# A hybrid attention and mLSTM block: GpSimd's weight work in pieces of 256 columns, fixed orders before the first feed-forward product and at the embedding gate, and a padding of 56 floats

## The chip, the cores and the metric

The kernel runs on one core of one Trainium2 chip. The metric is the device time of one execution in microseconds (us), the median of several runs. A core has five engines that are programmed apart and wait for each other by semaphores: TensorE (PE, with its weight loads shown as PEld), VectorE (DVE), ScalarE (ACT), GpSimd (POOL) and SyncE (SP), which issues transfers.

## The reference

One transformer block over 512 tokens of 1024 features, in float32. What matters here is its second half:

```python
merged = sigmoid(gate_a) * (y_a @ w_up_a) + sigmoid(gate_b) * (y_b @ w_up_b)
h = layer_norm(ALPHA * h + merged @ w_out, ln1_g, ln1_b)
ff = square(relu(h @ w_ff1)) @ w_ff2            # 1024 -> 4096 -> 1024
r = ALPHA * h + ff
r = r + sigmoid(r @ w_ple_gate) * (p @ w_ple_proj)   # the embedding gate
h = layer_norm(r, ln2_g, ln2_b)
```

Before it stand the input projection, a sparse attention with rotary embeddings, and an mLSTM, which give `y_a` and `y_b`.

## The kernel before

Every float32 product is made of three products of rounded halves. A weight or an activation `w` is cast to a high part (`wh`, on ScalarE), the low part is the difference `w - wh` (on VectorE or GpSimd: `split`, L110 to L112, and the last lines of `load_w`, L134), and `mm3` (L140 to L143) adds high x high (L141), high x low (L142) and low x high (L143) in one PSUM bank. So each tile of weights brings a transfer into a raw tile (`raw_tile`, three buffers), a cast on ScalarE, a subtraction on VectorE or GpSimd, and only then can L142 or L143 run on it.

The program has stages, one after the other on TensorE: input projection, attention and gates (to about 220 us), mLSTM (307), up projections with `merged`, here `m` (353), the output projection (`po`, weights `wo`, eight tiles in two halves `hh`) with the first layer norm and with transposes of the normed rows (`h_factors`, PSUM tiles `hps`) (405), the projection of `p` (`ple_projection`, PSUM tiles `ppw`, eight of 128x512, copied to `pws`) (418), the first feed-forward product (`ff1`, PSUM tiles `pf`, to 583), the second one (`ff2`, L1074, to 737), the embedding gate (`gate_product`, PSUM tiles `pg`, weights `wpg`, eight tiles) and the second layer norm.

Both feed-forward products use a fast scheme of seven products for eight blocks. `ff1` needs sums of blocks of the weights (`sums`, made by four GpSimd operations for each raw tile, L805 to L808 in `left_factors`), which are split into `w1h` and `w1l` like the weights, and sums of blocks of the normed rows, split into `hcH` and `hcL` by `put` in `h_factors`, L757 to L771. Its matmuls have the 128x128 blocks of `w1h` and `w1l` as stationary operands and 256 columns of `hcH` and `hcL` as moving ones. At the end of `ff2`, six GpSimd additions bring `e16` into `r` (L1110).

In the embedding gate `gate_inputs(i)` transposes the rows of block `i` (PSUM tiles `rps`) and splits them into `rH` and `rL`, and `gate_product(i, hh)` multiplies them by half `hh` of the weights; `gated` (L1201 to L1203) then applies the tanh (`th`) on ScalarE and two operations on VectorE.

What sets the order on each engine: the code is written for a framework that schedules the instructions by a simulated time, so the order on an engine is not that of the code. `tc.issue_after(...)` holds instructions behind a named one; `queued` (its operations have line L996) holds elementwise work of `ff2` and the gate in a list of its own, given out in order between the matmuls. An engine runs its list strictly in order.

```python
    def split(src, hi, lo, lo_eng=None):
        se.copy(hi, src)
        (lo_eng or ve).tensor_sub(lo, src, f(hi))
...
    gate_product(0, 0)
    for k in range(4):
        load_gate(1, k)
    gate_inputs(2)
    gate_product(1, 0)
    gate_inputs(3)
    gate_product(2, 0)
```

## Time and profile before

| | |
|---|---|
| median of 3 runs | 798.66 us (798.2 to 801.0) |
| the profiled execution's own time | 799.72 us |
| its span, first to last instruction | 798.0 us |
| TensorE busy | 776.5 us, 97% |
| VectorE, ScalarE, GpSimd busy | 614.1, 421.9, 361.4 us |
| mean granted TensorE clock | 0.989 of full speed |

Busy time is the union of an engine's instructions; matmuls are pipelined, so a matmul's own duration is longer than the distance between two starts. A wait is the idle time of an engine before an instruction, with the instruction that ended it. The granted clock is what the chip's throttle gave TensorE, 1.00 for 2.4 GHz and 0.50 for 1.2 GHz; a value between them is a mean over a stretch.

### The profile page before, as it was taken

What the parts mean: (1) busy time and instruction counts of PE and PEld (TensorE: products, weight loads), DVE (VectorE), ACT (ScalarE), POOL (GpSimd) and SP (SyncE); (2) the same over time, 40 slices, a digit from 0 to 9 for tenths busy, and PEclk for the clock granted to TensorE, in tenths of its full rate; (3) what the DMA queues carried; (4) which work ended last, traced back from release to release, by engine and by line L of the source; (5) the groups of instructions that cost most, each with busy time, mean ns of one, the idle gap of its engine ahead of it and who ended that gap; (6) DMA issues with size and microseconds to landing.
All of it is one profiled execution on the core that took longest, in us unless ns stands there. A gap on an engine that the chain in (4) does not pass through costs nothing.

```text
span 798.0 us, 11974 instructions
## 1 busy us (share of the span) xinstructions
PE 776.5 (97%) x4374; PEld 672.6 (84%) x4374; DVE 614.1 (77%) x1069; ACT 421.9 (53%) x687; POOL 361.4 (45%) x419
## 2 busy tenths in 40 slices
PE   8999999999999999999998999999999999999895
PEld 7888888779978888877888999999988888888685
DVE  4558999964548986384887889879878988989556
ACT  4445566687656543342255666566655456455300
POOL 5645563433245536475256877767410101118200
PEclk9999999999999999999999999999999999999898
DMA  7433133222222102546043366733169799893402
GB/s 223 139 80 105 54 80 91 64 71 68 66 80 80 39 28 67 180 143 231 1 172 106 120 240 180 246 117 97 49 152 213 146 403 294 143 203 111 129 27 79
DMA packets 84980, 102.06 MB, mean 128 GB/s; under 512 B 6197, under 2 KB 58933, under 8 KB 83642
## 3 DMA queue, kind: packets, MB, share of 16 engines
q1 hardware_dynamic: 74826, 80.33, 31.5%
q0 software_dynamic: 7392, 14.68, 10.6%
q10 hardware_dynamic: 2704, 6.29, 2.4%
q8 instruction: 34, 0.56, 0.3%
q14 instruction: 24, 0.20, 0.1%
HBM read 92.90 MB, written 8.39 MB: 127 GB/s over the span
## 4 chain that ended last, share of the span: by engine, by line
PE 72%; DVE 15%; POOL 5%; ACT 3%; DMA 3%; issue 2%; SPq 0%; DVEq 0%; POOLq 0%; ACTq 0%
PE pf L1074 16%; PE pf L141 6%; PE pf L143 6%; PE pf L142 6%; DVE sc L347 3%; DVE m L346 3%; PE pg L143 2%; PE pg L142 2%; PE pg L141 2%; PE po L142 2%; PE po L143 2%; PE po L141 2%; POOL r L1110 2%; PE pu L141 1%; PE pu L143 1%
## 5 line engine op out<-in xcount | busy, mean ns | idle before, releaser
L141 PE MATMUL pf<-hcH,w1h 128*128 128x256 f32 x448 | 123.0, 284 | 2.8 <-DVE hcL L112 2.5
L142 PE MATMUL pf<-hcL,w1h 128*128 128x256 f32 x448 | 123.9, 283 | 0.0
L143 PE MATMUL pf<-hcH,w1l 128*128 128x256 f32 x448 | 117.8, 283 | 0.6 <-DVE w1l L112 0.6
L141 PEld LDWEIGHTS pf<-hcH,w1h 128*128 128x128 f32 x448 | 84.7, 191 | 3.4 <-DVE hcL L112 2.7
L142 PEld LDWEIGHTS pf<-hcL,w1h 128*128 128x128 f32 x448 | 85.3, 190 | 0.0
L143 PEld LDWEIGHTS pf<-hcH,w1l 128*128 128x128 f32 x448 | 81.6, 190 | 0.8 <-DVE w1l L112 0.8
L938 POOL DMA_DIRECT2D b<-in_w_ff x14 | 18.1, 1289 | 122.3 <-DVE wl L996 111.4
L134 POOL TENSOR_TENSOR wgl<-wgr,wgh 128x256 fp32r<-128x256 f32 x64 | 50.9, 826 | 49.3 <-ACT wgh L130 49.3
L996 DVE TENSOR_TENSOR wl<-b,wh 128x2048 fp32r<-128x2048 f32 x27 | 64.0, 2370 | 8.7 <-ACT wh L996 8.7
L1074 PE MATMUL pf<-wh,ah 128*128 128x512 f32 x224 | 60.2, 391 | 0.2 <-ACT wh L996 0.2
L1074 PE MATMUL pf<-wh,al 128*128 128x512 f32 x224 | 59.9, 390 | 0.0
L112 DVE TENSOR_TENSOR w1l<-w1r,w1h 128x256 fp32r<-128x256 f32 (+1 forms) x62 | 48.4, 805 | 12.9 <-ACT w1h L111 12.9
L1074 PE MATMUL pf<-wl,ah 128*128 128x512 f32 x224 | 55.4, 390 | 0.0
L996 ACT CAST wh<-b 128x2048 fp32r<-128x2048 f32 x27 | 51.4, 1904 | 1.7 <-DMA b<-in_w_ff 1.7
L141 PE MATMUL pg<-xH,wgh 128*128 128x512 f32 x128 | 51.0, 399 | 0.0
L143 PE MATMUL pg<-xH,wgl 128*128 128x512 f32 x128 | 51.0, 398 | 0.0
L142 PE MATMUL pg<-xL,wgh 128*128 128x512 f32 x128 | 50.9, 398 | 0.0
L1074 PEld LDWEIGHTS pf<-wh,al 128*128 128x128 f32 x224 | 42.1, 188 | 8.7
L1074 PEld LDWEIGHTS pf<-wh,ah 128*128 128x128 f32 x224 | 41.8, 188 | 9.0 <-ACT wh L996 0.6
L1074 PEld LDWEIGHTS pf<-wl,ah 128*128 128x128 f32 x224 | 42.0, 188 | 8.7
L112 DVE TENSOR_TENSOR w1l<-sums,w1h 128x1024 fp32r<-128x1024 f32 x32 | 47.2, 1479 | 1.7 <-ACT w1h L111 1.7
L111 ACT CAST w1h<-w1r 128x512 fp32r<-128x512 f32 x64 | 29.7, 510 | 32.7 <-PE pf L142 32.4
(363 smaller groups left out, 2245.7 us busy)
## 6 DMA issues: line engine op xcount, KB each, us to landing
w1r<-in_w_ff SPq DMA_DIRECT2D x64, 256.0 KB, 3.1
b<-in_w_ff POOLq DMA_DIRECT2D x14, 1024.0 KB, 9.2
wgr<-in_w_in SPq DMA_DIRECT2D x16, 512.0 KB, 3.8
b<-in_w_ff SPq DMA_DIRECT2D x8, 1024.0 KB, 7.8
wor<-in_w_out SPq DMA_DIRECT2D x8, 512.0 KB, 4.4
b<-in_w_ff ACTq DMA_DIRECT2D x4, 1024.0 KB, 11.8
wpgr<-in_w_ple_gate SPq DMA_DIRECT2D x8, 512.0 KB, 7.4
xrs<-in_x SPq DMA_DIRECT2D x4, 512.0 KB, 5.1
```

What stands on the lines that cost most here:

```text
L111: se.copy(hi, src)
L112: (lo_eng or ve).tensor_sub(lo, src, f(hi))
L134: (lo_eng or ge).tensor_sub(lo[:, k:k + n], raw[:, k:k + n], f(hi[:, k:k + n]))
L141: te.matmul(ps, sh, mh, start=first, stop=False, **kw)
L142: te.matmul(ps, sh, ml, start=False, stop=False, **kw)
L143: return te.matmul(ps, sl, mh, start=False, stop=last, **kw)
L346: ve.max(m8, sc)
L347: ve.match_replace(out=sc, in_to_replace=m8, in_values=sc, imm_value=NEG_TAKEN)
L938: return ge.dma_start(out=tl, in_=rows_of(g, w), accum_op=OP.add)
L996: order_of[engine] = getattr(engine, op)(*args, **kw)
L1074: mm = te.matmul(banks[n, s], (al if kind == 1 else ah)[:, q, tok], (wl if kind == 2 else wh)[:, q], start=fresh and kind == 0 and q == 0, ...
L1110: (ge.tensor_sub if c else ge.tensor_add)(rs, rs, e16[:, s])
```

## The change

Five things change.

1. GpSimd's subtractions and additions on weights are cut into pieces of at most 256 columns: `low` in `split` (`wo`, `wp` and the first `w1l`), the `wpg` subtractions in `load_gate` (VectorE's there into two of 512), the rotary addition, and the additions of `e16` to `r`.
2. `left_factors` is divided into `left_sums` (transfer and GpSimd's sums) and `left_factors` (casts and subtractions). The first pair of sums is requested before the last rows' output projection and lies in the pool `ln`; so does the raw tile `prw`, which leaves a raw buffer free.
3. In front of `ff1` the order is fixed: four ple projections, the splits of the sums, two ple projections, the last rows' transposes, two ple projections.
4. The embedding gate's weights for the second half are requested after `gate_inputs(3)`, and `gate_inputs` casts through `queued`.
5. A tile of 56 floats (224 bytes) per partition is placed in the pool of the factors. `w1h` and `w1l` begin at 224 modulo 256 bytes before and at 0 after; `hcH` and `hcL` stay at 192.

The diff, cut to these places:

```diff
         se.copy(hi, src)
-        (lo_eng or ve).tensor_sub(lo, src, f(hi))
+        low(lo_eng or ve, lo, src, hi)
+
+    def low(eng, lo, src, hi):
+
+        if eng is not ge:
+            return eng.tensor_sub(lo, src, f(hi))
+        w = src.shape[-1]
+        for j in range(src.shape[1]):
+            for c in range(0, w, 256):
+                o = slice(c, min(c + 256, w))
+                eng.tensor_sub(lo[:, j][..., o], src[:, j][..., o], f(hi[:, j][..., o]))
...
@@ -702,7 +715,7 @@
 
     g1, be1 = row("ln1_g", ln), row("ln1_b", ln)
 
-    norm = []
+    norm, normed = [], []
...
-    loads, sums_done = [], []
-
-    def left_factors(q, half, later=None):
+    loads = []
+
+    def left_sums(q, half, pl=None):
 
         raw = raw_tile([P, 2, 2, 256], "w1r")
         for j in range(2):
             loads.append(sy.dma_start(raw[:, j], ff1_rows[:, j, half, :, q * 256:(q + 1) * 256]))
         a11, a21, a12, a22 = (raw[:, j, :, i * P:(i + 1) * P] for j in range(2) for i in range(2))
-        sums = W1S.tile([P, 4, 2, P], F32, tag="sums", bufs=2, name="sums")
+        sums = (pl or W1S).tile([P, 4, 2, P], F32, tag="sums", bufs=2, name="sums")
         ge.tensor_add(sums[:, 0], a21, a22)
         ge.tensor_sub(sums[:, 2], a11, a21)
         ge.tensor_sub(sums[:, 1], sums[:, 0], a11)
-        sums_done.append(ge.tensor_sub(sums[:, 3], a12, sums[:, 1]))
+        ge.tensor_sub(sums[:, 3], a12, sums[:, 1])
+        return raw, a22, sums
+
+    def left_factors(raw, a22, sums, lo_eng=None, later=None):
+
         hi = W1S.tile([P, 7, 2, P], F32R, tag="w1h", bufs=2, name="w1h")
         lo = W1S.tile([P, 7, 2, P], F32R, tag="w1l", bufs=2, name="w1l")
         for o, src in ((slice(0, 2), raw[:, :, :, 0:P]), (2, a22)):
-            split(src, hi[:, o], lo[:, o], ge if q == order[0] and o != 2 else ve)
+            split(src, hi[:, o], lo[:, o], lo_eng if o != 2 else ve)
         if later is None:
             split(sums, hi[:, 3:7], lo[:, 3:7])
         else:
@@ -838,6 +856,7 @@
         first_norm(i)
         if i:
             h_factors({2: 0, 1: 2}[i])
+    sums = [left_sums(order[0], half, ln) for half in range(2)]
     out_projection(NT - 1, 0)
     pTH, pTL, wp = ple_inputs()
     out_projection(NT - 1, 1)
@@ -846,30 +865,36 @@
     first_norm(NT - 1)
     later = []
     with tc.issue_after(norm[0].ins), tc.issue_after(norm[1].ins):
-        factors = [left_factors(order[0], half, later) for half in range(2)]
+        factors = [left_factors(*a, ge, later) for a in sums]
+
+    ge.memset(W1S.tile([P, 56], F32, name="off"), 0.0)
     h_factors(1)
 
-    pwss = []
+    pwss, projected, stored = [], [], []
 
     def ple_projection(i, hh):
         ps = acc("ppw")
         tok = slice(i * P, (i + 1) * P)
-        half_product(ps, lambda k: pTH[:, k, tok], lambda k: pTL[:, k, tok], blocks(wp[hh:hh + 1]))
+        projected[:] = [half_product(ps, lambda k: pTH[:, k, tok], lambda k: pTL[:, k, tok], blocks(wp[hh:hh + 1]))]
         if i == 0:
             pwss.append(gtile("pws", F32))
         pws = pwss[hh][:, i]
-        se.copy(pws, ps)
+        stored[:] = [se.copy(pws, ps)]
         sy.dma_start(pwd[:, i, hh * 512:(hh + 1) * 512], pws)
 
     todo = [(i, hh) for hh in range(2) for i in range(NT)]
     for _ in range(4):
         ple_projection(*todo.pop(0))
-    h_factors(NT - 1)
-    with tc.issue_after(last_block[0].ins):
+    with tc.issue_after(normed[0].ins), tc.issue_after(stored[0].ins):
         for a in later:
             split(*a)
-    for _ in range(4):
+    for _ in range(2):
         ple_projection(*todo.pop(0))
+    with tc.issue_after(projected[0].ins):
+        h_factors(NT - 1)
+    with tc.issue_after(turned[0].ins):
+        for _ in range(2):
+            ple_projection(*todo.pop(0))
...
                 queued(ve, "tensor_add", e16[:, s], e16[:, s], ps)
                 for i, c in ((s, 1), (2 + s, 0), (2 + s, 1)):
-                    rs = r[:, i, c * 512:(c + 1) * 512]
-                    (ge.tensor_sub if c else ge.tensor_add)(rs, rs, e16[:, s])
+                    for o in (0, 256):
+                        rs = r[:, i, c * 512 + o:c * 512 + o + 256]
+                        (ge.tensor_sub if c else ge.tensor_add)(rs, rs, e16[:, s, o:o + 256])
...
         queued(se, "copy", w[:, 0], raw)
         eng = ge if n in (2, 3, 5, 7) else ve
-        queued(eng, "tensor_sub", w[:, 1], raw, f(w[:, 0]))
-
+        for j in range(2):
+            for o in (slice(0, 256), slice(256, 512)) if eng is ge else (slice(0, 512),):
+                queued(eng, "tensor_sub", w[:, 1, j, o], raw[:, j, o], f(w[:, 0, j, o]))
...
             transpose4(ps, r[:, i, :], kk * 4)
             v = ps.rearrange("p (k q) -> p k q", k=4)
-            split(v, rH[:, kk * 4:kk * 4 + 4, tok], rL[:, kk * 4:kk * 4 + 4, tok])
+            hi = rH[:, kk * 4:kk * 4 + 4, tok]
+            queued(se, "copy", hi, v)
+            ve.tensor_sub(rL[:, kk * 4:kk * 4 + 4, tok], v, f(hi))
 
     EARLY = P5, P3
     RAW_STEPS = (0, P3, 1), (0, P6, 1), (1, P2, 0), (1, P2, 1)
@@ -1215,11 +1244,11 @@
         layer_norm(end, r[:, i, :], pw[i], g2, be2, lambda c: sy.dma_start(out_d[tok, c], pw[i][:, c]), **kw)
 
     gate_product(0, 0)
-    for k in range(4):
-        load_gate(1, k)
     gate_inputs(2)
     gate_product(1, 0)
     gate_inputs(3)
+    for k in range(4):
+        load_gate(1, k)
     gate_product(2, 0)
     for i in range(3):
```

On ScalarE before the first feed-forward product, of the kernel before (`hps` and `b12` belong to the last rows' transposes, `sums` to the first weight's factors; the last row is the last cast for it):

```order
L861 COPY pws_4494<-ppw_4506 128x512
L761 COPY b12_4465<-hps0_4455 128x512
L111 CAST hcH_3983<-hps1_4456 128x4x128
L111 CAST w1h_4382<-sums_4377 128x1024
L111 CAST hcH_3983<-hps0_4455 128x4x128
L111 CAST w1h_4396<-sums_4391 128x1024
L861 COPY pws_4494<-ppw_4515 128x512
L111 CAST hcH_3983<-hps1_4456 128x4x128
L111 CAST hcH_3983<-hps2_4471 128x4x128
L111 CAST hcH_3983<-hps3_4472 128x4x128
```

and of the changed kernel:

```order
L111 CAST w1h_4414<-sums_4304 128x1024
L111 CAST w1h_4421<-sums_4312 128x1024
L882 COPY pws_4494<-ppw_4487 128x512
L882 COPY pws_4494<-ppw_4497 128x512
L775 COPY b12_4516<-hps0_4506 128x512
L111 CAST hcH_3986<-hps1_4507 128x4x128
L882 COPY pws_4494<-ppw_4534 128x512
L111 CAST hcH_3986<-hps0_4506 128x4x128
L882 COPY pws_4494<-ppw_4543 128x512
L111 CAST hcH_3986<-hps1_4507 128x4x128
L111 CAST hcH_3986<-hps2_4522 128x4x128
```

Both casts of `w1h` from `sums` stood between the casts of `hcH`; now they stand ahead of everything on the last rows, and two copies of projections stand between the `hcH` casts.

On ScalarE at the embedding gate, of the kernel before (`rH` from `rps` is the cast of transposed rows, two for each block of rows; `wpg` from `wpgr` that of gate weights):

```order
L111 CAST rH<-rps 128x4x128
L996 CAST wpg<-wpgr 128x1024
L111 CAST rH<-rps 128x4x128 x2
L996 CAST wpg<-wpgr 128x1024 x2
L700 DMA ln_grow<-in_ln_g 128x1024
L111 CAST rH<-rps 128x4x128
L700 DMA ln_brow<-in_ln_b 128x1024
L996 CAST wpg<-wpgr 128x1024
L1201 ACTIVATE th_7828<-pg_7803 128x512
L111 CAST rH<-rps 128x4x128 x2
L1201 ACTIVATE th_7891<-pg_7866 128x512
L111 CAST rH<-rps 128x4x128 x2
```

and of the changed kernel:

```order
L1021 CAST rH<-rps 128x4x128 x3
L713 DMA ln_grow<-in_ln_g 128x1024
L1021 CAST rH<-rps 128x4x128
L713 DMA ln_brow<-in_ln_b 128x1024
L1230 ACTIVATE th_7870<-pg_7845 128x512
L1021 CAST rH<-rps 128x4x128 x2
L1230 ACTIVATE th_7913<-pg_7888 128x512
L1021 CAST rH<-rps 128x4x128 x2
L1021 CAST wpg<-wpgr 128x1024 x3
L1230 ACTIVATE th_7984<-pg_7959 128x512
L1021 CAST wpg<-wpgr 128x1024
L1230 ACTIVATE th_8013<-pg_7988 128x512
```

The casts of `wpg` for the second half stood between those of `rH` and the tanh; now they follow the last of `rH`.

On TensorE at the start of the output projection, of the kernel before (`wo_4005` and `wo_4010` are the first two weight tiles, `po_4047` and `po_4073` the first two blocks of rows):

```order
L143 MATMUL po_4047<-wo_4005,mHL_3802 128x512
L141 MATMUL po_4047<-wo_4010,mHL_3857 128x512
L141 MATMUL po_4073<-wo_4005,mHL_3802 128x512
L142 MATMUL po_4073<-wo_4005,mHL_3802 128x512
L143 MATMUL po_4073<-wo_4005,mHL_3802 128x512
L141 MATMUL po_4073<-wo_4005,mHL_3802 128x512
L142 MATMUL po_4073<-wo_4005,mHL_3802 128x512
L143 MATMUL po_4073<-wo_4005,mHL_3802 128x512
L141 MATMUL po_4073<-wo_4010,mHL_3857 128x512
L142 MATMUL po_4047<-wo_4010,mHL_3857 128x512
L143 MATMUL po_4047<-wo_4010,mHL_3857 128x512
L141 MATMUL po_4047<-wo_4010,mHL_3857 128x512
```

and of the changed kernel (`wo_4008` and `wo_4013`, `po_4068` and `po_4094`):

```order
L152 MATMUL po_4068<-wo_4008,mHL_3805 128x512
L150 MATMUL po_4068<-wo_4013,mHL_3860 128x512
L151 MATMUL po_4068<-wo_4013,mHL_3860 128x512
L152 MATMUL po_4068<-wo_4013,mHL_3860 128x512
L150 MATMUL po_4068<-wo_4013,mHL_3860 128x512
L150 MATMUL po_4094<-wo_4008,mHL_3805 128x512
L151 MATMUL po_4094<-wo_4008,mHL_3805 128x512
L152 MATMUL po_4094<-wo_4008,mHL_3805 128x512
L150 MATMUL po_4094<-wo_4008,mHL_3805 128x512
L151 MATMUL po_4094<-wo_4008,mHL_3805 128x512
L152 MATMUL po_4094<-wo_4008,mHL_3805 128x512
```

The first product with the low part of the second weight tile (L142 before, L151 after, on `wo_4010` and `wo_4013`) stood behind seven products of the second block of rows; now it stands before them.

## Rows read from the trace of the kernel before

**Rows 1.** Page, part 1: busy time, share of the span and instructions of each engine:

```profile
PE 776.5 (97%) x4374; PEld 672.6 (84%) x4374; DVE 614.1 (77%) x1069; ACT 421.9 (53%) x687; POOL 361.4 (45%) x419
```

**Rows 2.** TensorE's waits over the whole span: waiting line, what it waited for, us in total, times, longest:

```profile
PE pf L141 <- DVE hcL L112: 2.5, 1, 2.5
...
PE pg L143 <- DVE rL L112: 1.9, 1, 1.9
...
PE po L142 <- DVE wo L112: 1.8, 1, 1.8
...
PE pg L141 <- ACT rH L111: 1.1, 1, 1.1
```

**Rows 3.** Windows, TensorE: from:to, length, busy us (instructions), granted clock, DMA share, GB/s:

```profile
363.80:367.20 3.40, 3.40 (x10) 0.50 0.79 296
369.00:384.00 15.00, 15.00 (x65) 1.00 0.43 139
421.80:426.00 4.20, 4.16 (x22) 0.59 0.72 233
430.00:480.00 50.00, 50.00 (x425) 1.00 0.51 167
600.00:700.00 100.00, 100.00 (x443) 1.00 0.93 240
754.10:760.00 5.90, 5.90 (x14) 0.52 0.00 0
789.30:798.00 8.70, 0.39 (x4) 0.76 0.16 60
```

**Rows 4.** Groups of GpSimd's instructions by form: busy us, mean ns, idle before:

```profile
L134 POOL TENSOR_TENSOR mvwl<-mvwr,mvwh 128x256 fp32r<-128x256 f32 x16 | 11.3, 735 | 18.5 <-ACT mvwh L130 14.7 <-PE ptp L440 3.8
...
L134 POOL TENSOR_TENSOR aqwl<-aqwr,aqwh 128x512 fp32r<-128x512 f32 x8 | 10.6, 1345 | 12.7 <-ACT aqwh L130 12.7
...
L112 POOL TENSOR_TENSOR wo<-wor,wo 128x1024 fp32r<-128x1024 f32 x6 | 14.3, 2398 | 9.5 <-ACT wo L111 9.5
```

**Rows 5.** Timeline, output projection: start us, duration us, engine, line, operation:

```profile
351.68 1.23 DVE L112 TENSOR_TENSOR wo<-wor,wo 128x1024 fp32r<-128x1024 f32 x1 [2.48 <-ACT wo L111]
...
353.65 0.47 PE L141 MATMUL po<-wo,mHL 128*128 128x512 f32 x1
...
354.71 2.40 POOL L112 TENSOR_TENSOR wo<-wor,wo 128x1024 fp32r<-128x1024 f32 x1 [3.10 <-ACT wo L111]
...
359.39 3.31 DVE L112 TENSOR_TENSOR wo<-wor,wo 128x1024 fp32r<-128x1024 f32 x1
```

**Rows 6.** Timeline, start of the first feed-forward product:

```profile
419.53 1.04 ACT L111 CAST w1h<-sums 128x1024 fp32r<-128x1024 f32 x1 [2.25 <-POOL sums L808]
...
421.84 0.58 PE L141 MATMUL pf<-hcH,w1h 128*128 128x256 f32 x1 [2.47 <-DVE hcL L112]
```

**Rows 7.** Timeline, embedding gate:

```profile
749.42 1.05 ACT L996 CAST wpg<-wpgr 128x1024 fp32r<-128x1024 f32 x1 [4.39 <-DMA wpgr<-in_w_ple_gate]
...
750.86 1.06 ACT L111 CAST rH<-rps 128x512 fp32r<-128x512 f32 x2
...
750.99 2.45 DVE L1202 SCALAR_TENSOR_TENSOR pw<-th,pw 128x512 f32<-128x512 f32 x1 [4.59 <-ACT th L1201]
...
753.37 0.68 DVE L112 TENSOR_TENSOR rL<-rps,rH 128x512 fp32r<-128x512 f32 x1
```

**Rows 8.** Chain that ended last, embedding gate: start us, duration us:

```profile
743.70 5.70 DMA wpgr<-in_w_ple_gate
```

**Rows 9.** Timeline, end of the second feed-forward product and first gate product:

```profile
716.98 2.29 DVE L996 TENSOR_TENSOR wl<-b,wh 128x2048 fp32r<-128x2048 f32 x1 [0.58 <-ACT wh L996]
...
720.55 13.63 POOL L1110 TENSOR_TENSOR r<-r,e 128x512 f32<-128x512 f32 x6 [10.48 <-DVE e L996]
...
728.40 3.38 DVE L996 TENSOR_TENSOR wl<-b,wh 128x2048 fp32r<-128x2048 f32 x1
...
737.41 0.48 PE L141 MATMUL pg<-wpg,rH 128*128 128x512 f32 x1
```

More of the change, by code (lines that the diff above doesn't have):

```diff
@@ L146, in transpose4 @@
         for k in range(4):
-            te.transpose(dst[:, k * P:(k + 1) * P], src[:, (k0 + k) * P:(k0 + k + 1) * P], ident)
+            t_ = te.transpose(dst[:, k * P:(k + 1) * P], src[:, (k0 + k) * P:(k0 + k + 1) * P], ident)
+        return t_
     ident = const.tile([P, P], F32, name="ident")
@@ L219, in rope @@
         d0, d1 = dst[:, :, 0, :], dst[:, :, 1, :]
-        eng.tensor_add(d0, t1.rearrange("p n a b -> p n (a b)"), t2.rearrange("p n a b -> p n (a b)"))
+        m = 4 if eng is ge else n
+        for k in range(0, n, m):
+            eng.tensor_add(d0[:, k:k + m], t1[:, k:k + m].rearrange("p n a b -> p n (a b)"),
+                           t2[:, k:k + m].rearrange("p n a b -> p n (a b)"))
         se.copy(d1, d0)
@@ L725, in layer_norm @@
                 ve.scalar_tensor_tensor(src[:, c], src[:, c], ag[:, 0:1], g[:, c], op0=OP.subtract, op1=OP.mult)
-                ve.scalar_tensor_tensor(dst[:, c], src[:, c], ag[:, 3:4], b[:, c], op0=OP.mult, op1=OP.add)
+                normed[:] = [ve.scalar_tensor_tensor(dst[:, c], src[:, c], ag[:, 3:4], b[:, c], op0=OP.mult, op1=OP.add)]
                 if done:
@@ L735, in half_product @@
         for k, (wh, wl) in enumerate(ws):
-            mm3(ps, sh(k), sl(k), wh, wl, k == 0, k == len(ws) - 1)
+            mm = mm3(ps, sh(k), sl(k), wh, wl, k == 0, k == len(ws) - 1)
+        return mm
     def blocks(ws):
@@ L741, in block_kernel @@
     hb = [hbp.tile([P, 4, 256], F32, name=f"hb{kk}") for kk in range(2)]
-    last_block = []
+    turned = []
     def h_factors(i):
@@ L753, in h_factors @@
         for kk in range(2):
-            transpose4(ps[kk], r[:, i, :], kk * 4)
+            turned[:] = [transpose4(ps[kk], r[:, i, :], kk * 4)]
         if i < 2:
@@ L770, in h_factors @@
         put(HT3, ps[1])
-        last_block[:] = [ve.tensor_sub(v3, hb[1][:, :, o], v2)]
+        ve.tensor_sub(v3, hb[1][:, :, o], v2)
         put(HT2, p2)
@@ L777, in ple_inputs @@
     def ple_inputs():
-        prw = raw_tile([P, NT, PLE], "prw")
+        prw = ln.tile([P, NT, PLE], F32, name="prw")
         sy.dma_start(prw, p_d.rearrange("(i p) c -> p i c", p=P))
@@ L883, in ff1 @@
     def ff1(q, acts):
-        ws = factors if q == order[0] else [left_factors(q, half) for half in range(2)]
+        ws = factors if q == order[0] else [left_factors(*left_sums(q, half)) for half in range(2)]
         pairs_ = ((A11, HB11), (S2, HT2), (S3, HT3), (S1, HT1), (A12, HB21), (A22, HT4), (S4, HB22))
```

## The prediction

> **What bounds the kernel now.** I read the profile in this order. First the page: TensorE is busy for 776.5 us, 97% of the span [rows 1], and waits little. So only three things can change the time: places where TensorE stands still, matmuls that run slower than their neighbours, and the two ends. Second, TensorE's own waits [rows 2]: three places hold nearly everything beyond the start-up: 1.8 us in the output projection (`po`), 2.5 us at the start of the first feed-forward product (`pf`), and 1.1 + 1.9 us in the embedding gate (`pg`). Third, the windows behind these places [rows 3]: each is followed by a stretch with a granted clock of 0.50 to 0.59, that is at 1.2 instead of 2.4 GHz for all or most of it. A stretch of length L at mean granted clock c does work that full speed does in L x c, so it loses L x (1 - c): 3.4 x 0.50 = 1.7 us in `po`, 4.2 x 0.41 = 1.7 us in `pf`, 5.9 x 0.48 = 2.8 us in `pg`. The three places therefore cost 3.5, 4.2 and 5.8 us, 13.5 in all, and this is the most that fixed orders can return. Fourth, the timelines of the three places, for their causes.
>
> **GpSimd's pieces.** An operation on 128x1024 takes 2398 ns, one on 128x512 1345, one on 128x256 735 undisturbed [rows 4]. Four pieces for one are 4 x 735 = 2940 ns, 0.54 us more; over 11 such tensors (6 `wo`, 1 `wp`, 4 `wpg`) 6 us, and 6 x (2 x 735 - 1345) = 0.75 us at the `r` additions. GpSimd is off the critical path, so this counts only where a product waits for a low part. What the pieces return shows in `po`: while GpSimd worked on one `wo` for some 2.4 us, VectorE's subtraction of another took 3.31 us against 1.23 undisturbed, and TensorE waited for it [rows 2, 5]. VectorE stands still there for about as long as GpSimd's whole instruction still has to run; with quarter pieces it should stand for one piece.
>
> **The output projection.** With pieces of about 0.74 us VectorE's `wo` ends some 1.5 to 2 us earlier, and the wait of 1.83 us goes, with its 1.7 us at half clock. But the new order puts the low part of the second `wo` eighth in the first product, where seven products of another block stood before. The product begins at 353.65 [rows 5], so this matmul, seven times 230 ns later [rows 3], comes at about 355.3; it reads 512 columns, that is two of GpSimd's pieces. GpSimd's operation begins at 354.71 [rows 5], so they end between 356.2 and 356.9, the latter if a VectorE operation of 0.68 us takes a turn in between [rows 4, 7]; a start 0.7 us earlier, with VectorE's work otherwise timed, is the low end. So a new wait of 0.2 to 1.6 us; I take 1.3, nearer to the end with turns, because rows 5 show them. No row says whether a wait of that length brings the half clock again; the one of 1.83 did [rows 2, 3], so I count half of its 1.7 us, 0.9. Term: -1.8 - 1.7 + 1.3 + 0.9 = -1.3, between -3.3 (wait 0.2, no half clock) and -0.2 (wait 1.6, half clock).
>
> **The start of `pf`.** ScalarE stands 2.25 us before the cast of `w1h` from `sums`, which waits for GpSimd's additions, and behind it in the same queue is the cast of `hcH` on which the next product rests [rows 6]. In the new order the additions are made long before (on GpSimd right after `wo`), both casts stand ahead of the last block's transposes, and the transposes stand in front of two ple projections (12 matmuls, 12 x 230 = 2.8 us [rows 3]) where only one covered them. What is late next is VectorE: two low parts of `w1l` now stand before the additions on the last block. They are 128x1024, so 1.23 us each [rows 5], and the first `hcL` comes 0.1 to 1.4 us behind the matmul that wants it; I take 0.6, because most of GpSimd's work that could lengthen them is then over. Term: -2.5 - 1.7 + 0.6 = -3.6, between -4.2 and -2.0.
>
> **The embedding gate.** `th` and the casts of `rH` stand on ScalarE behind a cast of `wpg` that waits 4.39 us for its weights; VectorE's `pw` then takes 2.45 us beside a GpSimd operation, and `rL` comes after it [rows 2, 7]. In the new order all casts of `rH` precede the casts of the second half's `wpg`, so both waits and the half clock behind them should go: -5.8. The price: the last `wpg` gets its buffer only when VectorE has made the fourth-last one's low part. Without waits the third product ends at about 755.4 (72 matmuls at 226 ns [rows 3] and transposes from 737.4 [rows 9]); the last weights' low part is first wanted some 30 matmuls later, at 762.1. Its buffer is free at about 753.3 (the second product and its transposes end at 749.6; then come two casts of `rH`, 1.06 us, that buffer's own cast, 1.05, and VectorE's two halves, 2 x 0.68 [rows 7]), its load takes up to 5.70 us [rows 8], its cast 1.05 [rows 7], the first two pieces 1.5: 761.6. That just fits; with turns of VectorE between the pieces it is up to 2 us late. I take half, 1.0. Term: -4.8, between -5.8 and -2.8.
>
> **The `r` additions at the end of `ff2`.** Six operations take 13.63 us and not 6 x 1.345 = 8.1, while VectorE's 128x2048 beside them takes 3.38 us: the two engines alternate [rows 4, 9]. Twelve pieces are 8.8 us; with the same VectorE work in between, they end up to 2.3 us later. The new order on VectorE puts one `rL` ahead of the wait for them, so the first gate product is not held by all of that. I take +0.7, between 0 and 3.
>
> **The end.** After the last matmul 8.7 us remain [rows 3], all of it VectorE's chain. In the new order two operations of the third block's norm stand inside the last block's; at 0.68 us each [rows 7] they add 0 to 1.4 us, and I take 0.7.
>
> **The padding.** It moves the tiles of the first weight's factors (`w1h`, `w1l`) to another place modulo 256 bytes, and the 1344 matmuls of `pf` read them. These take 50.00 / 425 = 117.6 ns each; full speed without any surplus would be about a quarter of what 512 columns take at half clock [rows 3]: there 5.90 us for 14 matmuls of 512 columns is 421 ns, a quarter of which is 105, a bound of 12.6 x 1344 = 16.9 us on any gain. No row shows the new place. The nearest is the spread between 512-column products that read other places: 225.7 ns (443 in 100 us) and 230.8 (65 in 15 us) [rows 3], 5.1 ns per matmul, or 1344 x 5.1 = 6.9 us either way. I take 0, since nothing in the rows says that this spread is one of places. The Trainium skill's page "SBUF — State Buffer" (SBUF: two separate sides) says that TensorE never waits on anyone for its port, which makes the padding worth nothing; the spread of 5.1 ns here neither shows nor excludes that. Its page "TensorE: Matmul & The Clock Gate" (Wait — 56ns, not 53.3ns?) gives columns / 2.4 GHz + about 2.5 ns back to back, 109.2 ns here; these rows do not agree (117.6), and a padding that removed the whole difference would return an estimated 1344 x 8.4 = 11.3 us.
>
> **The sum.** -1.3 - 3.6 - 4.8 + 0.7 + 0.7 + 0 = -8.3 us against the profiled execution's 799.72, so 791.4. That execution lies 1.06 above the median of 798.66, so 790.4 in the measure of the medians. The attention part is reordered slightly; I cost that at nothing, because the waits that count lie elsewhere [rows 2]; what hides it is that TensorE has other matmuls queued there, and without that cover it belongs to the slower case below. The ends of all terms together are -13.3 and -0.6; as they will not all fall on one side, this case's own range is 786 to 795.
>
> **Rivals.**
> - *The pieces are dear*: each of them loses a turn to VectorE, so the new wait in `po` is 1.6 us and brings the half clock back (+1.1, and 0.4 for a second wait there), the `r` pieces come 3 us late (+2.3) and the last `wpg` 2 us late with half clock behind it (+3.8). For it: rows 5 and 9 show turns. Against: VectorE has few operations of two tensors at these places. -8.3 + 7.6 = -0.7: 798.0.
> - *The padding costs*: +6.9, so 797.3.
> - *The padding pays*: -6.9, so 783.5.
> - *Slower*: the `r` additions become the bound. If each of the 12 pieces lost its turn to a whole 128x2048 operation (2.29 undisturbed [rows 9]), they would take 12 x (0.74 + 2.29) = 36 us and end at 756.8 instead of 734.2; the low parts of the third and fourth `wpg` stand behind them, wanted at 740.6, so TensorE would stand about 20 us: 810. It decides for slower once the chain ends later than about 748.6 (734.2, 2.2 of slack, 8.3 of gains, 4 more). Against: only about four such operations lie in those 13.6 us.
>
> **How the numbers follow.** A measurement of this kernel can tell about 0.5%, 4 us. Forecast 0.65 (790.4: faster); pieces dear 0.13 and padding costs 0.07 (both within 0.5%); padding pays 0.08 (faster); slower 0.07, which also holds waits that I do not see in the reordered attention part. So 0.73 / 0.20 / 0.07. The range 784 to 799 takes in the forecast's own range, the two cases near 798, and leaves out the slower case and half of the padding's gain.
>
> **What would show it.** Right: no waits above 0.5 us at the start of `pf` and in `pg`, a granted clock of 1.00 from 417 to 430 and from 750 to 766 (in the old times), `po` with one wait near 355 and none near 361, 1344 `pf` matmuls at 117 to 119 ns, the same 8.7 us at the end or up to 1.4 more. Wrong: `pf` below 115 or above 121 ns (the padding's case), or new waits of `pg` for the low part of `wpg` or for `r`.

## The result and the profile after

The changed kernel takes 791.81 us (median of 6 executions, 790.8 to 792.5) against 798.43 for the kernel before on the same chip: a ratio of 0.991, 95% interval 0.989 to 0.993. The forecast was 790.4 in a range of 784 to 799, faster. The profiled execution of after took 790.8 us with a span of 789.1, that of before 799.72 with 798.0, so the two traces differ by 8.9 us where the medians differ by 6.6; what follows splits the 8.9.

Part of this difference is in the execution of before that was profiled. The 77 executions of before that were timed beside the variants took 792.2 to 801.7 us: 792.2 to 795.1 in the six whose mean granted clock was 0.996 or 0.997 and 799.7 to 800.9 in the twelve where it was 0.989 or less. The profiled one, at 0.989, holds all three stretches at half clock, which the prediction puts at 1.7 + 1.7 + 2.8 = 6.2 us. The six executions of after lie at 0.996 to 0.998. So between executions with a like clock the two kernels are some 1 to 2 us apart (791.81 and, in e9, 793.15 against a median of 794.0 of those six), and the rest of the 6.6 goes with the half clock, which the changed kernel has more seldom. Which waits the quick executions of before had is not known, since none was profiled.

TensorE's waits in the trace of after, which answer to [rows 2]:

```profile
engine line waited for: us in total, times, longest us
...
PE pf L150 <- DVE u L927: 2.0, 2, 1.5
PE po L151 <- POOL wo L122: 1.8, 1, 1.8
PE pf L150 <- DVE hcL L117: 1.1, 1, 1.1
PE hps L156 <- DVE r L739: 0.8, 1, 0.8
...
PE pf L150 <- ACT hcH L111: 0.4, 1, 0.4
```

No wait of `pg` is left. The wait of `po` has changed its cause (GpSimd's `wo`, not VectorE's) and kept its size. The 2.5 us at the start of `pf` have become 1.1 and 0.4, and there is a new line, transposes that wait for `r`. The wait of `pf` products for VectorE's `u` inside the product was 0.3 us before.

Windows of after, TensorE (from:to, length, busy us and instructions, granted clock, DMA share, GB/s), which answer to [rows 3]:

```profile
354.00:357.20 3.20, 1.51 (x7) 1.00 0.85 296
357.20:367.20 10.00, 9.85 (x41) 1.00 0.81 289
...
417.30:424.00 6.70, 5.19 (x39) 1.00 0.72 251
424.00:469.00 45.00, 45.00 (x384) 1.00 0.37 122
471.00:479.60 8.60, 8.60 (x79) 1.00 0.78 263
...
553.50:579.00 25.50, 25.50 (x227) 1.00 0.13 42
734.90:747.00 12.10, 12.10 (x61) 1.00 0.36 132
747.00:760.00 13.00, 13.00 (x63) 1.00 0.12 40
```

Every window behind a wait has a clock of 1.00; the three stretches at half clock are gone. The fourth to sixth of these windows hold `pf` matmuls alone, without a wait. A matmul lasts some 280 ns, 2.4 times the distance of two starts, so 2.4 of each count began before the window: 45.00 / 381.6 = 117.9 ns, but 8.60 / 76.6 = 112.3 and 25.50 / 224.6 = 113.5 ns. Taken from start to start over all undisturbed pairs (1320 of 1343), the distances are 117.8 ns in some stretches and 113.3 in others, 115.7 on average, against 118.3 before.

The first starts of the stages in the two traces give where the 8.9 us come from:

| stretch | before, us | after, us | difference |
|---|---|---|---|
| to the first `po` | 353.65 | 353.72 | +0.1 |
| first `po` to first `pf` | 64.14 | 63.58 | -0.6 |
| first `pf` to first of `ff2` | 165.06 | 162.89 | -2.2 |
| `ff2` to first `pg` | 154.56 | 154.67 | +0.1 |
| first to last `pg` | 52.00 | 45.86 | -6.1 |
| after the last matmul | 8.59 | 8.38 | -0.2 |

### The profile page after: what moved, and what is told of

It is laid out like the page before. It is cut to its first block, busy times and chain, and to the rows that moved or that the text cites. A ratio compares the mean times of both kernels' runs of the same rounds, so it can differ in the third digit from the quotient of the medians.

```text
span 789.1 us, 12032 instructions
## 1 busy us (share of the span) xinstructions
PE 770.0 (98%) x4374; PEld 665.9 (84%) x4374; DVE 609.2 (77%) x1073; ACT 422.3 (54%) x687; POOL 380.3 (48%) x464
## 5 line engine op out<-in xcount | busy, mean ns | idle before, releaser
L150 PE MATMUL pf<-hcH,w1h 128*128 128x256 f32 x448 | 120.6, 281 | 4.2 <-DVE u L927 2.0
L151 PE MATMUL pf<-hcL,w1h 128*128 128x256 f32 x448 | 120.6, 279 | 0.0
L152 PE MATMUL pf<-hcH,w1l 128*128 128x256 f32 x448 | 111.6, 279 | 0.2 <-DVE w1l L117 0.2
L151 PEld LDWEIGHTS pf<-hcL,w1h 128*128 128x128 f32 x448 | 84.5, 189 | 0.0
L152 PEld LDWEIGHTS pf<-hcH,w1l 128*128 128x128 f32 x448 | 78.6, 188 | 0.7 <-DVE w1l L117 0.6
L151 PE MATMUL pg<-xL,wgh 128*128 128x512 f32 x128 | 50.9, 398 | 0.0
L117 DVE TENSOR_TENSOR w1l<-sums,w1h 128x1024 fp32r<-128x1024 f32 x32 | 45.2, 1416 | 0.0
L143 POOL TENSOR_TENSOR wul<-wur,wuh 128x128 fp32r<-128x128 f32 x64 | 33.9, 561 | 20.7 <-ACT wuh L140 13.0
```

Source lines behind the costliest of these rows:

```text
L117: return eng.tensor_sub(lo, src, f(hi))
L143: (lo_eng or ge).tensor_sub(lo[:, k:k + n], raw[:, k:k + n], f(hi[:, k:k + n]))
L150: te.matmul(ps, sh, mh, start=first, stop=False, **kw)
L151: te.matmul(ps, sh, ml, start=False, stop=False, **kw)
L152: return te.matmul(ps, sl, mh, start=False, stop=last, **kw)
```

## The experiments

Ten variants were run, one of them twice, and the changed kernel once more, in three groups of four (e1 to e4, e5 to e8, e9 to e12); each group also timed the kernel before. "Over the changed kernel" is said against 791.81 us, its first measurement, and 793.15, its second (e9); where a span is given, these are its two ends.

**The padding alone and the gate's order.** First, the changed kernel without the padding:

```diff
-    ge.memset(W1S.tile([P, 56], F32, name="off"), 0.0)
```

> The changed kernel without the tile of 56 floats: w1h and w1l return to 224 modulo 256 bytes, all orders and pieces stay. Theory (the place sets the distance of the pf matmuls): the undisturbed distance between two pf starts returns from 115.7 ns to 118.3, no stretch of 113.3 ns is left, and the time rises by 1343 x 2.6 ns = 3.5 us less what shorter waits in ff1 give back (up to 1.5): +2 to +3.5 us. Rival (the distance comes from where the stream pauses, not from the place): stretches of 113 ns stay and the time moves by less than 1 us.

Measured: 795.75 us (794.38 to 796.44), ratio to before 0.997 (0.995 to 0.999); no stretch of 113 ns, mean 118.3. The theory of the place holds, at its upper end: 2.6 to 3.9 us over the changed kernel.

The kernel before with the padding alone:

```diff
         factors = [left_factors(order[0], half, later) for half in range(2)]
+    ge.memset(W1S.tile([P, 56], F32, name="off"), 0.0)
```

> The kernel before with the tile of 56 floats alone: w1h and w1l go to 0 modulo 256, nothing else changes. Theory (the place): the undisturbed distance of the pf matmuls falls from 118.3 to between 113.3 and 117.8 ns by stretches, the waits in po, at the start of pf and in pg stay at 1.8, 2.5 and 3.0 us, and the time falls by 0.7 to 6 us, some 3 likely. Rival (the gain needs the new orders): 118.3 ns stays and the time is that of the kernel before within 1 us.

Measured: 796.94 us, ratio 0.9985 (0.996 to 1.001), so by time alone not told from no change. The distance of `pf` fell to 114.1 ns on average, as the theory says; in the trace 1316 undisturbed pairs then save 5.5 us, but the whole product takes 162.47 instead of 164.94 us between its first and last start. TensorE then waits more inside `pf`: 1.2 us for VectorE's `u` and 0.8 for `hcH`, where before it was 0.3 and nothing. The shorter distance reaches the time only in part, because the work of VectorE and ScalarE on which `pf` waits is not faster.

The same tile with 8 floats:

```diff
-    ge.memset(W1S.tile([P, 56], F32, name="off"), 0.0)
+    ge.memset(W1S.tile([P, 8], F32, name="off"), 0.0)
```

> The changed kernel with 8 floats in place of 56: w1h and w1l at 192 modulo 256, the place that hcH and hcL have. Theory A (equal places of the two operands are the quick ones, as 227 ns against 233 with 512 columns suggests): all pf matmuls near 113 ns, time 2 to 3 us under the changed kernel. Theory B (only a start at 0 is quick): 118 ns, time 2 to 3.5 us over it. Theory C (equal places are the slow ones, as 12 matmuls of 256 columns in the mLSTM with 122 ns suggest): 122 ns, 6 us or more over it.

Measured: 796.27 us, ratio 0.998 (0.997 to 1.000). 119.9 ns, the same in nearly all pairs, and 3.1 to 4.5 us over the changed kernel: theory A falls; the distance lies between those of B and C, so equal places are slow here, by less than C had it.

The gate's order of before in the changed kernel, pieces kept:

```diff
     gate_product(0, 0)
+    for k in range(4):
+        load_gate(1, k)
     gate_inputs(2)
     gate_product(1, 0)
     gate_inputs(3)
-    for k in range(4):
-        load_gate(1, k)
...
-            hi = rH[:, kk * 4:kk * 4 + 4, tok]
-            queued(se, "copy", hi, v)
-            ve.tensor_sub(rL[:, kk * 4:kk * 4 + 4, tok], v, f(hi))
+            split(v, rH[:, kk * 4:kk * 4 + 4, tok], rL[:, kk * 4:kk * 4 + 4, tok])
```

> The changed kernel with the embedding gate's order of before (requests of the second half's weights before gate_inputs(2), gate_inputs with split), the pieces kept. Theory (the order makes the gate's gain): the waits for rH and rL of 1.1 and 1.9 us return, with a stretch at half clock behind them, and the time rises by 4 to 6 us. Rival (the pieces make it, because VectorE's pw no longer stands beside a whole GpSimd operation): at most 1.5 us of wait returns, no half clock, and the time rises by under 2 us.

Measured: 796.72 us, ratio 0.997 (0.995 to 0.999): 3.6 to 4.9 us over the changed kernel. From the timeline of this variant at the gate (start us, duration us, engine, line, operation):

```profile
750.21 1.04 ACT L1021 CAST wpg<-wpgr 128x1024 fp32r<-128x1024 f32 x1 [3.87 <-DMA wpgr<-in_w_ple_gate]
751.16 1.07 ACT L111 CAST rH<-rps 128x512 fp32r<-128x512 f32 x2
...
751.78 0.69 DVE L117 TENSOR_TENSOR rL<-rps,rH 128x512 fp32r<-128x512 f32 x1 [3.27 <-ACT rH L111]
...
751.80 0.50 PE L150 MATMUL pg<-wpg,rH 128*128 128x512 f32 x1 [1.80 <-ACT rH L111]
```

and its window behind that wait:

```profile
751.00:756.00 5.00, 4.20 (x11) 0.67 0.00 0
```

The wait for `rH` is back (1.80), with a stretch at half clock. The wait for `rL` is not: in this variant the first `pw` ran at 747.09 (0.68 us), before ScalarE stood still, where before it began at 750.99, took 2.45 us, and `rL` stood behind it [rows 7]. So the variant does not bring back the whole order of before on VectorE, and the rival's cause could not show here; that pieces give nothing at the gate under the new order is shown by e7 below. In time the theory of the order holds.

**Other places, the pieces, and the order in front of `pf`.** Two more sizes of the tile, 24 and 40 floats (the edit is that of e3):

> The changed kernel with 24 floats in place of 56: w1h and w1l at 128 modulo 256, that is 64 below the 192 of hcH and hcL, as 0 is 64 above it. So far the pf distance was 113.3 or 117.8 ns by stretches at 0, a mixture of 116 and 122 (mean 118.3) at 224, and 119.9 throughout at 192. Theory D (what counts is how far the two places lie apart in 64-byte steps): as at 0, 113.3 and 117.8 by stretches, the time of the changed kernel within 2 us. Theory E (only 0 is quick): 118 to 120 ns, 3 to 6 us over the changed kernel.

> The same with 40 floats: w1h and w1l at 64 modulo 256, 128 away from hcH and hcL. The 256-column products of the input projection, which also lie 128 apart (64 and 192), take 118.2 ns. Theory D: 118 ns throughout, 3 us over the changed kernel. Theory E: the same. A third possibility (any place that is not within 32 bytes has the quick state) would show 113.3 ns in stretches and the changed kernel's time.

Measured: 24 floats 794.46 us (0.996, 0.994 to 0.998), 1.3 to 2.7 us over the changed kernel, with 113.3 ns in 82 of 1321 pairs and 117.8 in nearly all the rest; 40 floats 794.9 us (0.997, 0.995 to 1.000), 1.8 to 3.1 over it, mean 118.9, spread from 115 to 123. Neither theory is whole: at 128 both values of 0 appear (D), but the quick one hardly ever, and the time lies between D's (within 2) and E's (3 to 6). At 64 D and E were not to be told apart; the mean is near what both say, the spread is not. The third possibility falls.

All GpSimd work whole again (`low` takes a tensor in one operation, no loops in the rotary addition, the `r` additions and `wpg`):

```diff
-        if eng is not ge:
+        if eng is not None:
             return eng.tensor_sub(lo, src, f(hi))
...
-                    for o in (0, 256):
-                        rs = r[:, i, c * 512 + o:c * 512 + o + 256]
-                        (ge.tensor_sub if c else ge.tensor_add)(rs, rs, e16[:, s, o:o + 256])
+                    rs = r[:, i, c * 512:(c + 1) * 512]
+                    (ge.tensor_sub if c else ge.tensor_add)(rs, rs, e16[:, s])
...
-        for j in range(2):
-            for o in (slice(0, 256), slice(256, 512)) if eng is ge else (slice(0, 512),):
-                queued(eng, "tensor_sub", w[:, 1, j, o], raw[:, j, o], f(w[:, 0, j, o]))
+        queued(eng, "tensor_sub", w[:, 1], raw, f(w[:, 0]))
```

> The changed kernel with all GpSimd work whole again (wo, wp, w1l, wpg, the rotary addition, the r additions; VectorE's wpg whole too), orders and padding kept. Theory of the prediction (pieces are worth about 1 us, in po): the wait for VectorE's wo near 361 returns (1 to 2 us) with or without half clock, the wait near 355 for GpSimd's wo stays or grows to 2 to 3 us because the first low part now comes with the whole operation; po takes 2 to 4 us more, the r additions end 1 us earlier; sum +1 to +4 us. Rival (pieces matter most at the gate and in ff1): waits of over 1 us in pg.

Measured: 792.19 us, ratio 0.995 (0.992 to 0.997): the time of the changed kernel. Its waits:

```profile
PE pf L150 <- DVE u L927: 1.9, 3, 1.5
PE po L151 <- DVE wo L117: 1.7, 1, 1.7
...
PE hps L156 <- DVE r L739: 1.0, 1, 1.0
```

The wait for VectorE's `wo` is back at 360.63 (1.70), the one for GpSimd's at 355 is gone, and `po` takes 49.61 us between its first and last start against 49.55. So here the pieces exchange one wait for another of the same size. In `pg` no wait returns, so with the new order there the pieces have nothing to add. The wait that the first theory named came, its +1 to +4 us did not, and the rival's waits in `pg` did not come either: on the time both theories fall.

The order in front of `pf` as before, with the sums late and `prw` in a raw buffer:

```diff
-    sums = [left_sums(order[0], half, ln) for half in range(2)]
...
-        prw = ln.tile([P, NT, PLE], F32, name="prw")
+        prw = raw_tile([P, NT, PLE], "prw")
...
-        factors = [left_factors(*a, ge, later) for a in sums]
+        factors = [left_factors(*left_sums(order[0], half), ge, later) for half in range(2)]
...
-    with tc.issue_after(normed[0].ins), tc.issue_after(stored[0].ins):
+    h_factors(NT - 1)
+    with tc.issue_after(last_block[0].ins):
         for a in later:
             split(*a)
-    for _ in range(2):
-        ple_projection(*todo.pop(0))
-    with tc.issue_after(projected[0].ins):
-        h_factors(NT - 1)
-    with tc.issue_after(turned[0].ins):
-        for _ in range(2):
-            ple_projection(*todo.pop(0))
+    for _ in range(4):
+        ple_projection(*todo.pop(0))
```

> The changed kernel with the order of before in front of pf (sums requested late, prw in a raw buffer, the last rows' transposes after four projections in the code, splits of the sums behind the last rows' work), pieces, padding and gate order kept. Theory of the prediction (the order is worth the wait of 2.5 us and the half clock behind it, less the new wait of 1.5 us): waits of 2 to 3 us at the start of pf, a stretch at half clock behind them, +2 to +3.5 us. Rival (with pieces GpSimd's sums are early enough anyway): waits under 1.5 us there, no half clock, within 1 us of the changed kernel.

Measured: 787.7 us (786.55 to 789.9), ratio 0.989 (0.986 to 0.992): faster than the changed kernel by 4.1 us, where both expectations had it slower or equal. Its waits and the windows around the longest:

```profile
PE pf L150 <- ACT hcH L111: 2.3, 1, 2.3
PE po L151 <- POOL wo L122: 0.8, 1, 0.8
```

```profile
418.00:421.00 3.00, 0.74 (x7) 1.00 0.86 244
421.00:430.00 9.00, 9.00 (x82) 1.00 0.23 77
```

The wait of before is there (2.3), yet no half clock follows it in this execution, and there is no wait for `r`.

**The two parts of that order on one chip.** The changed kernel, e8's kernel, and the two halves of its edit (only the order of before, or only the late sums):

> The changed kernel once more, for a comparison on one chip with the three below. All theories: 0.989 to 0.993 of the kernel before, 1343 pf matmuls at 113.3 or 117.8 ns by stretches, waits of about 1.1 us at the second pf product and about 1 us for r at the last rows' transposes.

> The kernel of e8 once more (sums late and the order of before in front of pf). Theory (e8's gain is real and comes from the stretch between po and pf): 3 to 5 us under the changed kernel on the same chip, no wait for r at the last rows' transposes, one wait of 2 to 2.5 us at the second pf product, with a stretch at half clock behind it only in some executions. Rival (e8 was a chance of the pf distance and of the chip): within 1.5 us of the changed kernel.

> The changed kernel with the order of before in front of pf, but the sums still requested early and prw still in the other pool. Theory A (the early sums cost, because GpSimd then works on the next factors' sums beside VectorE's norm of the last rows): the wait for r stays, time of the changed kernel within 1.5 us. Theory B (the fixed order costs): no wait for r over 0.3 us, and the time of e10 within 1.5 us, or less, since the wait for the sums (2.3 us) goes too.

> The changed kernel with the sums requested late as before, but the new order in front of pf. Theory A: no wait for r, the time of e10 within 1.5 us or better. Theory B: the wait for r and that at the second pf product stay, with the sums' own wait added: the changed kernel's time or up to 3 us more.

| | sums early | sums late |
|---|---|---|
| new order | e9: 793.15 (791.69 to 794.77) | e12: 791.37 (790.52 to 793.05) |
| order of before | e11: 791.66 (790.46 to 793.45) | e10: 789.83 (787.41 to 790.38) |

In the order e9, e12, e11, e10 the ratios to the kernel before are 0.994 (0.992 to 0.997), 0.993 (0.990 to 0.995), 0.993 (0.991 to 0.996) and 0.990 (0.987 to 0.993). All six executions of e10 lie under all eight of e9, as all six of e8 lay under all six of the changed kernel. The waits of the four, in the order e9, e10, e11, e12:

```profile
PE hps L156 <- DVE r L739: 1.5, 2, 1.2
PE pf L150 <- DVE hcL L117: 1.5, 2, 1.1
```

```profile
PE pf L150 <- ACT hcH L111: 2.2, 1, 2.2
PE pf L150 <- DVE u L923: 1.8, 3, 0.9
PE po L151 <- POOL wo L122: 1.8, 1, 1.8
```

```profile
PE hps L156 <- DVE hcL L117: 2.0, 3, 1.2
...
PE ppw L150 <- ACT pws L883: 0.8, 1, 0.8
```

```profile
PE pf L150 <- DVE u L926: 2.9, 5, 0.8
...
PE pf L150 <- ACT hcH L111: 2.3, 1, 2.3
```

e9 came out at 0.994, just outside the 0.989 to 0.993 expected; e10 is as its theory says, 3.3 us under e9. With the sums early (e9, e11) TensorE waits before `pf`, at the transposes and projections; with the sums late (e10, e12) it waits once at the second `pf` product. But the wait for `r` that theory A has stay in e11 is not there: it needs the early sums and the new order together, and under the order of before waits for `hcL` and `pws` stand in its place. On the time neither theory is whole: each half alone gives about half of the 3.3 us, 1.5 and 1.8, though some executions of e11 and e12 lie among those of e9. Why the new order costs with the sums late (e12 against e10) is open. Their profiled executions can't tell it: they are 0.35 us apart, both have half clock behind the wait at `pf` (0.76 from 420 to 427 us in e10, 0.62 from 420.5 to 425 in e12; e10 behind its wait in `po` as well), and e12 has more waits inside `pf` for `u` (five, 2.9 us, against three, 1.8), which the order there does not touch directly.

How the early sums make the wait for `r` shows in two timelines (the rows of SyncE, SPq, run from the first of two issues to the end of the second), that of after:

```profile
377.45 21.28 SPq L672 DMA_DIRECT2D wpr<-in_w_ple_proj  x2
...
401.84 1.05 ACT L111 CAST wp<-wpr 128x1024 fp32r<-128x1024 f32 x1 [3.09 <-DMA wpr<-in_w_ple_proj]
...
402.92 1.23 DVE L117 TENSOR_TENSOR wp<-wpr,wp 128x1024 fp32r<-128x1024 f32 x1 [1.19 <-ACT wp L111]
...
405.26 0.68 DVE L847 SCALAR_TENSOR_TENSOR r<-r,po 128x512 f32<-128x512 f32 x1
...
407.90 2.42 DVE L738 SCALAR_TENSOR_TENSOR r<-r,lag,ln_grow 128x512 f32<-128x512 f32 x2
...
410.92 1.23 DVE L739 SCALAR_TENSOR_TENSOR r<-r,lag,ln_brow 128x512 f32<-128x512 f32 x1
...
412.68 1.32 DVE L739 SCALAR_TENSOR_TENSOR r<-r,lag,ln_brow 128x512 f32<-128x512 f32 x1
...
414.05 0.66 PE L156 MATMUL hps<-ident,r 128*128 128x128 f32 x4 [0.84 <-DVE r L739]
```

and that of e10, with the sums late:

```profile
374.18 3.15 SPq L672 DMA_DIRECT2D wpr<-in_w_ple_proj  x2
...
405.09 0.68 DVE L848 SCALAR_TENSOR_TENSOR r<-r,po 128x512 f32<-128x512 f32 x1
...
407.90 1.41 DVE L738 SCALAR_TENSOR_TENSOR r<-r,lag,ln_grow 128x512 f32<-128x512 f32 x2
...
411.05 2.38 DVE L739 SCALAR_TENSOR_TENSOR r<-r,lag,ln_brow 128x512 f32<-128x512 f32 x2
```

The last two operations (L739) take about as long in both, 1.23 and 1.32 us after and 2.38 for the two in e10, where 0.68 each is usual for this size [rows 7]; GpSimd's `w1l` pieces run beside them in both, so these are not the difference. Two things are. First, the early sums hold two of the three raw buffers, so the second transfer into `wpr` is issued by 398.7 us instead of 377.3, its cast waits 3.09 us for it, and VectorE stands 1.19 us before `wp`'s low part, with the addition of the last `po` behind it in its list: that addition starts 1.6 us after the end of the last `po` matmul (3.3 in e9, 3.4 in e11), against 0.7 in e8, e10 and e12. Second, the two operations of L738 take 2.42 us (2.37 and 2.39 in e9 and e11) beside GpSimd's sums for the next factors, against 1.41 in e8, e10 and e12. Together the norm of the last rows ends 10.3 us behind the last `po` matmul (12.0 and 11.2), against 9.0 to 9.1 in the three others. The transposes of the last rows, which the new order has put one projection earlier, come before `r` is ready. That the buffer is the cause and not only goes with it was not tried by itself: no run has early sums with one more raw buffer.

## Why the prediction was right, and where it was not

Time, sign and range were right. Of the signs it named, the clock, `pg`, `po` and the end came as said; at the start of `pf` a wait of 1.1 us stayed where none above 0.5 was to be, and the `pf` matmuls, at 115.7 ns on average with stretches of 113.3, lie outside the 117 to 119 of the right case. Term by term, from the two traces:

- **Output projection**, -1.3 predicted. Between its first and last start `po` takes 49.55 us instead of 51.15, -1.6. The new wait is there, as said, at the low part of the second `wo`:

```profile
354.97 5.14 POOL L122 TENSOR_TENSOR wo<-wor,wo 128x256 fp32r<-128x256 f32 x4 [3.19 <-ACT wo L111]
...
355.46 2.33 DVE L690 SCALAR_TENSOR_TENSOR mHL<-m,mHL 128x512 fp32r<-128x512 f32 x2
...
357.29 0.50 PE L151 MATMUL po<-wo,mHL 128*128 128x512 f32 x1 [1.78 <-POOL wo L122]
```

  It is 1.78 us, over my upper end of 1.6: the four pieces took 5.14 us, since VectorE had more than one operation to take turns with. In exchange no half clock followed, of which I had counted half. That the wait for VectorE's `wo` went is the pieces' doing (e7). The gain of 1.6 is not: waits of nearly the same length stand in both traces, and only the half clock went. With whole operations (e7) it did not follow either, and in e10, whose `po` has the pieces, it followed a wait of 1.80 us and `po` took 50.89. So that this term came out is in part luck of the execution.
- **Start of `pf`**, -3.6 predicted. Waits of 1.1 + 0.4 took the place of 2.5, and the half clock went; by the starts, the first 8 us of `pf` lose 2.38 us against the undisturbed distance instead of 4.25, a difference of -1.9. The wait for `r` in front of it, 0.8, was not foreseen: -1.1. The step that failed is "the additions are made long before": they are, but at the cost of VectorE's norm, which ended 10.3 us behind `po` where it ends 9.0 to 9.1 behind it with the sums late, and which I had looked at only for `hcL`. e8 and e10 show that the kernel is better off without this part.
- **Embedding gate**, -4.8 predicted, -6.1 measured. Mechanism right, price too high: the last `wpg` was not late.

```profile
755.51 1.05 ACT L1021 CAST wpg<-wpgr 128x1024 fp32r<-128x1024 f32 x1 [1.56 <-DMA wpgr<-in_w_ple_gate]
...
756.64 2.82 POOL L1021 TENSOR_TENSOR wpg<-wpgr,wpg 128x256 fp32r<-128x256 f32 x4 [1.86 <-ACT wpg L1021]
```

  It was ready at 759.5 and, some 29 matmuls after the third product's end at 753.2, wanted near 760; its transfer had landed at 755.5, 3.5 us sooner than my sum had it.
- **The `r` additions**, +0.7 predicted, +0.1 for the stretch to the first `pg`. The twelve took 14.5 us (13.6 before [rows 9]), and as said VectorE had an `rL` ahead of the wait.
- **The end**, +0.7 predicted, -0.2 measured; the two operations of the third block's norm fitted beside the last products.
- **The padding**, 0 predicted, between -6.9 and +6.9. Here the size was wrong, and half of the gain that the rival "the padding pays" had came in: e1 and e2 show a change of place to change the distance of the `pf` matmuls, 118.3 to 115.7 ns in the trace of after, 1320 x 2.6 = 3.4 us. The time gains less where VectorE does not keep up: in the trace of after the waits and restarts inside `pf` behind its first 8 us grew from 1.8 to 5.0 us. So `pf` as a whole, its start included, gives -2.2. The nearest rows I had taken, 512-column products, were misleading: by the kernel's layout the quickest of them, `ff2` (226.8 ns from start to start, others 228 to 233), has both operands at 192, while with 256 columns equal places are slow (119.9, e3). No run moved the places of 512-column products.

Two ends that the prediction gives do not follow from its own terms: 1.4 us late at the start of `pf` makes -2.8, not -2.0, and 2 us late at the gate -3.8, not -2.8. The forecast does not hang on them.

That -8.3 came so near to -8.9 in the traces is partly chance: the gate gave 1.3 us more than its term, `po` 0.3 and the two small terms 1.5 more, the start of `pf` with the wait in front of it 2.5 less, and the padding's 3.4 us, not in the sum, were spent on new waits inside `pf`. The single effects on the time (padding 2.6 to 3.9 us, gate's order 3.6 to 4.9, pieces none, the order in front of `pf` with its early sums -3.3 to -4.1) do not add up to the whole of 6.6 by themselves: each was measured by taking it out of the changed kernel. Half clock, which follows a wait in one execution and not in another, may be a part of the rest; no run shows how large a part.

The version of e8 and e10 (changed kernel with the early sums and the order in front of `pf` taken back) beats both kernels: 0.989 and 0.990 of the time of before in two measurements, 3.3 to 4.1 us under the changed kernel.

## What to carry to other kernels

Look at what a moved piece of work does to the engine beside it, not only at whom it serves: GpSimd's sums were off the critical path and early, and still went with a later norm on VectorE, since they held buffers that another tile's transfer needed and ran beside VectorE's operations. Cutting an operation into pieces shortened the other engine's (VectorE's `wo` from 3.31 to 1.21 us) and lengthened its own (GpSimd's `wo` from 2.40 to 5.14), so it pays only where the one is waited for and the other is not. One execution with three stretches at half clock is a poor base for a sum: time the kernel before often enough to see how its times spread, and with which granted clock. Where TensorE is bound by its own stream, compare the distance between starts too: where an operand lies was worth about as much here as a wait (2.6 to 3.9 us), and one line (a tile of some floats) tells it.

## What the runs showed of the hardware that was not expected

**The place of the stationary operand.** With the moving operand at 192 modulo 256 bytes and 256 columns, the undisturbed distance of the `pf` matmuls was, by the place of `w1h` and `w1l` (the tile of floats also moves what else lies behind it in their pool, such as the later sums; no run moved one tile alone):

| place | kernel | distance, ns | mean |
|---|---|---|---|
| 0 | changed kernel, e2, e4, e7 to e12 | 113.3 or 117.8 by stretches | 113.5 to 115.9 |
| 64 | e6 | spread from 115 to 123 | 118.9 |
| 128 | e5 | 117.8, in one stretch 113.3 | 117.5 |
| 192 | e3 | 119.9 nearly throughout | 119.9 |
| 224 | before, e1 | spread from 115 to 123, most near 116 and 122 | 118.3 |

At 0 the value mostly stays the same over hundreds of matmuls and changes where TensorE has waited or is held up. The same program shows both: e8 has mostly 113.3 ns from 421 to 498 us and 117.8 from there on, e10 113.3 almost throughout (mean 113.5). The Trainium skill's page "SBUF — State Buffer" (SBUF: two separate sides) says that TensorE never waits on anyone for its port. The runs neither bear that out nor contradict it: the distance goes with the place of an operand and is not always the same, but no run shows what TensorE waits for there.

**The half clock behind a wait.** A wait of 2.3 us at the second `pf` product was followed by 1.00 in e8 and, in the same program, one of 2.2 us by 0.76 over the next stretch in e10 (and one of 2.5 at the same place by 1.00 in e2):

```profile
420.00:427.00 7.00, 4.78 (x29) 0.76 0.51 164
```

In `po` a wait of 1.70 us was followed by 1.00 in e7 and one of 1.78 by 1.00 after, but one of 1.83 by 0.50 before [rows 3], and in e10, with the same code in `po` as after, one of 1.80 by 0.57:

```profile
357.00:361.00 4.00, 4.00 (x12) 0.57 0.57 141
```

So the price of a wait of this length is itself, or itself and some 1.7 us more (4.00 x 0.43 in the last row), and one trace can't tell which it will be.
